# Second attention: where the selection's mask joins each head's bias, a matmul into the logits or an accumulating transfer into the bias

## The chip, the cores and the metric

The kernel runs on one core of one Trainium2 chip. The metric is the device time of one execution, in microseconds; three runs of the kernel before gave 1299.54 to 1299.88 us, median 1299.84.

## The reference, cut to what matters

The model is two layers of a decoder trunk over 512 positions and 1024 features. Layer 0 mixes with a stick-breaking attention, layer 1 with a sparse attention (the "second attention" here), and a gated MLP with a short convolution follows each. In the second attention an indexer scores every key for every query, the 128 best keys are selected, and 16 heads attend to these alone, all with the same keys, with a relative bias of their own and the same selection:

```python
_, sel = lax.top_k(isc, topk)
valid = sel <= t[None, :, None]
...
logits = jnp.einsum('bqhd,bqkd->bqhk', qb, kg) * scale
bias = rel_bias[t5_bucket(t[None, :, None] - sel)]
logits = logits + jnp.swapaxes(bias, -1, -2).astype(jnp.float32)
logits = jnp.where(valid[:, :, None, :], logits, NEG)
p = jax.nn.softmax(logits, axis=-1)
return jnp.einsum('bqhk,bqkd->bqhd', p, vg)
```

The kernel gathers nothing: it computes the logits against all keys up to the query's block, adds the bias, and adds -1e30 where a key is not selected, so the softmax gives those keys 0.

## The kernel before, in words

**Tiles.** Queries lie in four blocks of 128 (index j, 0 to 3); block j sees the first (j + 1) * 128 keys, so a head's logits are four tiles of 128, 256, 384 and 512 columns, kept side by side in one tile `L` of 1280 columns (`LOFF` gives the offsets 0, 128, 384, 768). Most matmuls are done three times, with weights and activations each split into a high and a low part (`hi`, `lo`), which ScalarE (ACT) makes by a copy and VectorE (DVE) by a subtraction.

**The mask.** While the queries of the first 12 heads are projected, DVE takes the top 128 keys by repeated max and match-replace (`topk_steps`), and at the end (L1205) writes `maskb`: bf16, 0 or -1e30, the same for all heads.

**The bias.** The relative bias of a head depends only on the distance between query and key, so a row of 640 numbers per head lies in DRAM (`rb`), and `load_bias` (L1325) reads it with overlapping rows, one DMA on the queue of SyncE (SP) of 128 x 512 floats, into a tile `th`. `th` holds the bias in reversed order of keys, and is read backwards. There are two `th` buffers in a pool that opens with the attention part.

**One head.** `logits(h, j)` (L1336) makes tile `z`: three matmuls of queries and keys and, as the fourth (L1346), the identity `ident_b` times `maskb`, which adds the mask in PSUM. `softmax(h, j)` (L1348) has DVE compute `L = z * rq + bias` (L1354) and the negated row maximum `nm` (L1356). `expo(h, j)` has ACT take the exponential, with the row's sum. `transposed(h, .)` turns `L` on TensorE (PE) in three pieces (tile `tr`), copied out to `pT` by ACT or DVE. `weighted(h)` multiplies two heads' weights with the values (`av`), once for every pair of heads; `pair_sums`, `pair_scale`, `pair_hi`, `pair_lo` scale that pair's result and split it. There are two PSUM banks for `z`, two for `tr`, one for the small products (`x`), three for projections.

**The order.** The program's order is written by hand, and every engine runs its own instructions in it. The loop over heads h does the logits and the softmax of head h + 1 between the transposes of head h: first `logits(h+1, 0)` and `(h+1, 1)`, then (even h above 0) `weighted(h-2)`, the first transposes of head h, some steps of other work (`fill`: projections of the last four heads' queries, then half of the output projection, with their splits as `events`), `logits(h+1, 2)`, more transposes, `logits(h+1, 3)`, the last transposes, and at the end of the head the load of the bias of head h + 2. In the text, tile (n, j) means block j of head n.

**The weights.** All weights come through a ring of six buffers of 128 x 1024 floats, pool `raws`. `fetch` (through `chunk_raw`, L178) issues their loads on SP's queue, one chunk ahead of the split. SP's queue is in order: a transfer that waits for its buffer holds up all that stand behind it.

**GpSimd (POOL)** does, before the attention part, the low halves of 12 splits (`wlo`), and nothing in it.

Of the kernel before, what the change touches and what calls it, by code (L numbers as in the profile page):

```python
# [9 lines left out]
F32 = mybir.dt.float32  # L10
F32R = mybir.dt.float32r
BF = mybir.dt.bfloat16
AF = mybir.ActivationFunctionType
OP = mybir.AluOpType
# [4 lines left out]
D = 1024  # L19
S = 512  # L20
P = 128
KT = D // P
QT = S // P
# [4 lines left out]
HEADS = 16  # L28
# [10 lines left out]
LATE_STEPS = [2, 3, 2, 3, 3, 3, 3, 3, 3, 3, 5, 5, 5, 5, 5, 8]  # L39
AHEAD = 2  # L40
FETCH = 1
IDXFILL = [1, 1, 1, 0, 1, 1, 1, 1]

TRP = [[(0, 0)], [(1, 0), (3, 384)], [(2, 0)]]
TRW = [512, 512, 256]
LOFF = [0, 128, 384, 768]
LW = 1280
# [71 lines left out]
def kernel_body(ctx, tc, xT, wst, cst, smalls, crow, ccol, relb, onehot, outT):  # L119
    nc = tc.nc  # L120
    act, dve, pe, pool = nc.scalar, nc.vector, nc.tensor, nc.gpsimd
# [927 lines left out]
    def dsa_layer(l, first, man):  # L1049
        with ExitStack() as st:  # L1050
# [233 lines left out]
            with ExitStack() as sa:  # L1284
# [34 lines left out]
                def fill(n):  # L1319
                    for _ in range(n):  # L1320
                        next(filler, None)
                        if events:
                            events.pop(0)()

                def load_bias(h):  # L1325
                    th = ths[h] = ap.tile([P, S], F32, name="th", bufs=2)
                    ov = rb[h:h + 1, 0:1]
                    nc.sync.dma_start(th, bass.AP(tensor=ov.tensor, offset=ov.offset, ap=[[1, P], [1, S]]))

                def begin(h):  # L1330
                    L = ap.tile([P, LW], F32, name="L")
# [5 lines left out]
                def logits(h, j):  # L1337
                    qh, ql = Q[h]
                    ns = (j + 1) * P
                    qs = slice(j * P, ns)  # L1340
                    ls = slice(LOFF[j], LOFF[j] + ns)
                    z = heads[h][4][j] = ptile([P, S], "z", "z")
                    pe.matmul(z[:, :ns], lhsT=qh[:, qs], rhs=kph[:, :ns], start=True, stop=False)
                    pe.matmul(z[:, :ns], lhsT=ql[:, qs], rhs=kph[:, :ns], start=False, stop=False)
                    pe.matmul(z[:, :ns], lhsT=qh[:, qs], rhs=kpl[:, :ns], start=False, stop=False)
                    pe.matmul(z[:, :ns], lhsT=ident_b, rhs=maskb[:, ls], start=False, stop=True)  # L1346

                def softmax(h, j):  # L1348
                    L, nm, sum_, rv, z = heads[h]
                    z = z.pop(j)  # L1350
                    ns = (j + 1) * P
                    ls = slice(LOFF[j], LOFF[j] + ns)
                    c = h * QT + j
                    dve.scalar_tensor_tensor(L[:, ls], z[:, :ns], rq[:, c:c + 1], ths[h][:, :ns][:, ::-1],  # L1354
                                             op0=OP.mult, op1=OP.add)
                    dve.tensor_reduce(nm[:, j:j + 1], L[:, ls], axis=AX.X, op=OP.max, negate=True)  # L1356

                def expo(h, j):
                    L, nm, sum_ = heads[h][:3]
                    ls = slice(LOFF[j], LOFF[j] + (j + 1) * P)  # L1360
                    act.activation(L[:, ls], L[:, ls], AF.Exp, bias=nm[:, j:j + 1], accum_out=sum_[:, j:j + 1])
# [74 lines left out]
                for j in range(QT):  # L1436
                    logits(0, j)
                    fill(1)
                    softmax(0, j)
                    expo(0, j)  # L1440
                rvb = None

                def sums(h):
# [4 lines left out]
                for h in range(HEADS):  # L1448
                    n = h + 1
                    more = n < HEADS  # L1450
                    values = h % 2 == 0 and h > 0
                    if more:
                        begin(n)
                        for j in range(2):
                            logits(n, j)
                        softmax(n, 0)
                        expo(n, 0)
# [25 lines left out]
                    if more:  # L1483
                        softmax(n, 3)
                        expo(n, 3)
                        if n + 1 < HEADS:
                            load_bias(n + 1)
                    else:
                        pair_scale(rvb)
                    fill(LATE_STEPS[h] - LATE_STEPS[h] // 2)  # L1490
# [124 lines left out]
```

## Time and profile before

| | us |
|---|---|
| median of three runs | 1299.84 |
| span of the profiled execution (first to last instruction) | 1297.7 |
| the second attention's loop over heads, about | 771 to 903 of the span |
| PE busy over the span | 1280.5 |
| DVE busy over the span | 930.7 |
| ACT busy over the span | 591.4 |
| POOL busy over the span | 35.8 |

The profile is of one execution. The page's own times are in us from the start of its span; the runs' times are 2.1 us longer than that span. A row of the timeline gives the start, the duration, the engine, the line of the kernel, the operation, "out<-in", the shapes and, in brackets, how long the engine had stood idle before it and what released it. PEld is PE's loading of weights, which overlaps PE's matmuls. Matmuls are pipelined: what one costs is read from the start of the next, not from its own duration. In the chain of waits each row is a start, a length and the instruction that the end of the program waited for at that time.

### The profile page before, as it was taken

Reading aid. Unit: us, or ns where it says so; the run is one execution under the profiler, and the core shown is the slowest. Engines: PE = TensorE matmul, PEld = TensorE weight load, DVE = VectorE, ACT = ScalarE, POOL = GpSimd, SP = SyncE. Lnnn points to the kernel's source line nnn. Section 1 sums busy time; section 2 is a strip of 40 time slices with the busy share of each in tenths; the row PEclk is TensorE's granted clock in tenths of the full one; section 3 lists DMA queues with packets and bytes.
Section 4 is the critical chain, followed back from the end, with each engine's and each line's share of the span. In section 5 each row is a group of like instructions: output and inputs, shape, how many; then the busy total and the mean of one; then the engine's idle time right before and its main releaser. Section 6 shows DMA issues by size and latency. Waiting matters only on the chain.

```text
span 1297.7 us, 18005 instructions
## 1 busy us (share of the span) xinstructions
PE 1280.5 (99%) x6988; PEld 1066.7 (82%) x6988; DVE 930.7 (72%) x1532; ACT 591.4 (46%) x1049; POOL 35.8 (3%) x27
## 2 busy tenths in 40 slices
PE   8999999999999999999999999999999999999998
PEld 5978787898888888888987777777998888888888
DVE  5888988778777877875778877777876456456643
ACT  5476666454323423442555346565554234234430
POOL 0000000000000000000102410000000000000000
PEclk9999999999999999999999999999999999999999
DMA  9644444324575575654213211213222422423221
GB/s 375 207 130 131 144 126 125 126 66 124 199 252 191 175 246 190 192 175 142 80 52 91 88 31 51 65 58 122 82 83 78 129 86 74 129 91 97 73 90 66
DMA packets 50613, 163.23 MB, mean 126 GB/s; under 512 B 5808, under 2 KB 8624, under 8 KB 50528
## 3 DMA queue, kind: packets, MB, share of 16 engines
q1 hardware_dynamic: 50096, 161.30, 38.6%
q8 instruction: 55, 0.90, 0.3%
q10 hardware_dynamic: 432, 0.79, 0.2%
q14 instruction: 30, 0.25, 0.1%
HBM read 159.92 MB, written 2.14 MB: 125 GB/s over the span
## 4 chain that ended last, share of the span: by engine, by line
PE 92%; DVE 3%; ACT 2%; DMA 1%; issue 1%; SPq 0%; DVEq 0%; ACTq 0%
PE pt_u L249 11%; PE pt_u L250 11%; PE pt_u L251 11%; PE pt_d L250 5%; PE pt_d L249 5%; PE pt_d L251 5%; PE pt_first L250 2%; PE pt_l L249 2%; PE pt_first L251 2%; PE pt_first L249 2%; PE pt_l L250 2%; PE pt_l L251 2%; PE pt_q L249 2%; PE pt_q L251 2%; PE pt_q L250 2%; PE pt_qk L249 2%
## 5 line engine op out<-in xcount | busy, mean ns | idle before, releaser
L209 ACT ACTIVATE whi<-raw 128x1024 fp32r<-128x1024 f32 (+1 forms) x206 | 205.2, 1002 | 118.8 <-PE pt_d L251 89.6
L249 PE MATMUL pt_u<-hhi,whi 128*128 128x512 f32 x640 | 249.4, 390 | 0.0
L250 PE MATMUL pt_u<-hhi,wlo 128*128 128x512 f32 x640 | 249.2, 389 | 0.0
L251 PE MATMUL pt_u<-hlo,whi 128*128 128x512 f32 x640 | 249.1, 389 | 0.0
L217 DVE TENSOR_TENSOR wlo<-raw,whi 128x1024 fp32r<-128x1024 f32 (+1 forms) x194 | 223.7, 1154 | 17.7 <-ACT whi L209 16.8
L985 ACT ACTIVATE y<-pt_u,sm 128x512 f32<-128x512 f32 x80 | 62.2, 777 | 188.3 <-PE pt_u L251 188.3
L249 PEld LDWEIGHTS pt_u<-hhi,whi 128*128 128x128 f32 x640 | 120.2, 188 | 26.0 <-issue 1.1
L251 PEld LDWEIGHTS pt_u<-hlo,whi 128*128 128x128 f32 x640 | 120.2, 188 | 24.9
L250 PEld LDWEIGHTS pt_u<-hhi,wlo 128*128 128x128 f32 x640 | 120.2, 188 | 24.7
L986 DVE SCALAR_TENSOR_TENSOR y<-pt_u,sm,y 128x511 f32<-128x511 f32 x80 | 59.9, 749 | 97.0 <-ACT y L985 96.8
L249 PE MATMUL pt_d<-acthi,whi 128*128 128x512 f32 x288 | 112.1, 389 | 0.0
L251 PE MATMUL pt_d<-actlo,whi 128*128 128x512 f32 x288 | 112.1, 389 | 0.0
L250 PE MATMUL pt_d<-acthi,wlo 128*128 128x512 f32 x288 | 112.1, 389 | 0.0
L258 DVE SCALAR_TENSOR_TENSOR raw<-raw,cond 128x1024 f32<-128x1024 f32 x88 | 106.6, 1217 | 3.8 <-DMA raw<-wst 3.8
L360 DVE SCALAR_TENSOR_TENSOR x<-pt_d,mod,x 128x512 f32<-128x512 f32 x48 | 36.0, 750 | 72.8 <-PE pt_d L251 72.8
L233 ACT ACTIVATE acthi<-y 128x512 fp32r<-128x512 f32 x44 | 27.8, 632 | 105.4 <-DVE y L1004 105.4
L249 PE MATMUL pt_first<-hhi,whi 128*128 128x256 f32 (+1 forms) x224 | 68.6, 306 | 0.1
L250 PE MATMUL pt_first<-hhi,wlo 128*128 128x256 f32 (+1 forms) x224 | 67.2, 300 | 0.9 <-DVE wlo L217 0.8
L251 PE MATMUL pt_first<-hlo,whi 128*128 128x256 f32 (+1 forms) x224 | 67.0, 299 | 0.0
L249 PEld LDWEIGHTS pt_d<-acthi,whi 128*128 128x128 f32 x288 | 54.1, 188 | 11.2
L251 PEld LDWEIGHTS pt_d<-actlo,whi 128*128 128x128 f32 x288 | 54.1, 188 | 11.2
L250 PEld LDWEIGHTS pt_d<-acthi,wlo 128*128 128x128 f32 x288 | 54.1, 188 | 11.2
(253 smaller groups left out, 2661.3 us busy)
## 6 DMA issues: line engine op xcount, KB each, us to landing
raw<-wst SPq DMA_DIRECT2D x250, 512.0 KB, 3.7
raw<-wst SPq DMA_DIRECT2D x48, 384.0 KB, 3.0
th<-rb SPq DMA_DIRECT2D x16, 256.0 KB, 3.5
ada<-wst SPq DMA_DIRECT2D x4, 512.0 KB, 6.3
outT<-x SPq DMA_DIRECT2D x16, 128.0 KB, 1.7
x<-xT SPq DMA_DIRECT2D x5, 256.0 KB, 5.0
x<-xT ACTq DMA_DIRECT2D x3, 256.0 KB, 3.9
cond<-crow SPq DMA_DIRECT2D x1, 512.0 KB, 10.5
```

Source lines behind the costliest of these rows:

```text
L209: act.activation(hi[:, :n], raw[:, :n], AF.Copy)
L217: engine.tensor_sub(lo[:, :n], raw[:, :n], hi[:, :n].bitcast(F32))
L233: act.activation(hi, src, AF.Copy)
L249: pe.matmul(out, lhsT=whi, rhs=ahi, start=start, stop=False)
L250: pe.matmul(out, lhsT=wlo, rhs=ahi, start=False, stop=False)
L251: pe.matmul(out, lhsT=whi, rhs=alo, start=False, stop=stop)
L258: dve.scalar_tensor_tensor(raw, raw, 1.0, cond, op0=OP.mult, op1=OP.mult, accum_out=dst)
L360: dve.scalar_tensor_tensor(x[f][:, c], pt, mod[l][:, g * KT + f:g * KT + f + 1], x[f][:, c], op0=OP.mult, op1=OP.add)
L985: act.activation(y, pt, AF.Identity, scale=cw[2], bias=sm[:, b + S_CB + c:b + S_CB + c + 1])
L986: dve.scalar_tensor_tensor(y[:, 1:], pt[:, :S - 1], cw[1], y[:, 1:], op0=OP.mult, op1=OP.add)
```

## The change

For heads 2 to 15 the mask is no longer added by PE. After head 0's exponentials, `store_mask` has ACT copy the mask, reversed and as floats, into two tiles, and stores them in DRAM (`maskd`). The bias of such a head is loaded in four pieces, one for each block j, into two tiles of the ring `raws` (blocks 0 to 2 in one of 768 columns, block 3 in one of 512), so that it lies as the mask lies; then two DMAs on POOL's queue add `maskd` onto the two tiles as they transfer. Heads 0 and 1 keep the matmul, and their bias, 128 x 512, comes into the ring as well. The pool of two `th` buffers is gone. The load for head h + 2 stands at the beginning of head h, not at its end.

```diff
+PEMASK = 2
...
+                maskd = dp.tile([P, LW], F32, name="maskd")
+
+                def halves_of():
+                    return [raws.tile([P, D], F32, name="th", tag="raw")[:, :w] for w in (LOFF[3], S)]
+
+                def store_mask():
+                    for t, c0 in zip(halves_of(), (0, LOFF[3])):
+                        for j in (0, 1, 2) if c0 == 0 else (3,):
+                            ns = (j + 1) * P
+                            act.activation(t[:, LOFF[j] - c0:LOFF[j] - c0 + ns], maskb[:, LOFF[j]:LOFF[j] + ns][:, ::-1], AF.Copy)
+                        nc.sync.dma_start(maskd[:, c0:c0 + t.shape[1]], t)
+
                 def load_bias(h):
-                    th = ths[h] = ap.tile([P, S], F32, name="th", bufs=2)
+                    th = ths[h] = halves_of() if h >= PEMASK else halves_of()[1:]
                     ov = rb[h:h + 1, 0:1]
-                    nc.sync.dma_start(th, bass.AP(tensor=ov.tensor, offset=ov.offset, ap=[[1, P], [1, S]]))
+                    for j in range(QT) if h >= PEMASK else (3,):
+                        ns = (j + 1) * P
+                        t = th[-1] if j == 3 else th[0][:, LOFF[j]:LOFF[j] + ns]
+                        nc.sync.dma_start(t, bass.AP(tensor=ov.tensor, offset=ov.offset, ap=[[1, P], [1, ns]]))
+                    if h >= PEMASK:
+                        pool.dma_start(th[0], maskd[:, :LOFF[3]], accum_op=OP.add)
+                        pool.dma_start(th[1], maskd[:, LOFF[3]:], accum_op=OP.add)
...
-                    pe.matmul(z[:, :ns], lhsT=qh[:, qs], rhs=kpl[:, :ns], start=False, stop=False)
-                    pe.matmul(z[:, :ns], lhsT=ident_b, rhs=maskb[:, ls], start=False, stop=True)
+                    pe.matmul(z[:, :ns], lhsT=qh[:, qs], rhs=kpl[:, :ns], start=False, stop=h >= PEMASK)
+                    if h < PEMASK:
+                        pe.matmul(z[:, :ns], lhsT=ident_b, rhs=maskb[:, ls], start=False, stop=True)
...
-                    dve.scalar_tensor_tensor(L[:, ls], z[:, :ns], rq[:, c:c + 1], ths[h][:, :ns][:, ::-1],
+                    dve.scalar_tensor_tensor(L[:, ls], z[:, :ns], rq[:, c:c + 1], bias_of(h, j),
...
+                store_mask()
                 rvb = None
...
                     values = h % 2 == 0 and h > 0
+                    if n + 1 < HEADS:
+                        load_bias(n + 1)
                     if more:
                         begin(n)
...
                         expo(n, 3)
-                        if n + 1 < HEADS:
-                            load_bias(n + 1)
```

**PE, in the loop of head 6**, from the small product `ssq` to the logits of tile (7, 2). First before, then now:

```order
L1091 MATMUL ssq<-ecols,q_7760 128x1 x4
L1343 MATMUL z<-kph,qh 128x128
L1344 MATMUL z<-kph,ql 128x128
L1345 MATMUL z<-kpl,qh 128x128
L1346 LDWEIGHTS ident_b
L1346 MATMUL z<-maskb,ident_b 128x128
L1343 MATMUL z<-kph,qh 128x256
L1344 MATMUL z<-kph,ql 128x256
L1345 MATMUL z<-kpl,qh 128x256
L1346 LDWEIGHTS ident_b
L1346 MATMUL z<-maskb,ident_b 128x256
L1372 MATMUL tr<-cons,L 128x128 x4
```

The same stretch of PE after the change, where the lines of the code have moved on by some 26:

```order
L1092 MATMUL ssq<-ecols,q_7793 128x1 x4
L1369 MATMUL z<-kph,qh 128x128
L1370 MATMUL z<-kph,ql 128x128
L1371 MATMUL z<-kpl,qh 128x128
L1369 MATMUL z<-kph,qh 128x256
L1370 MATMUL z<-kph,ql 128x256
L1371 MATMUL z<-kpl,qh 128x256
L1399 MATMUL tr<-cons,L 128x128 x4
```

Of PE nothing moved but the mask's weight loads and matmuls, 56 of each, which are gone.

**SP, at the start of the attention part**, from the first bias on (`th` with a number is one tile; heads 0, 1, 2, 3 in this order; in brackets the engines and DMA semaphores that the transfer waits for). First before, then now:

```order
L1328 DMA th_7175<-rb_102 128x512 [waits DVE_49,DMAHW1_49,PE_49,Activation_49]
L1328 DMA th_7177<-rb_102 128x512 [waits DMAHW2_49]
L1328 DMA th_7289<-rb_102 128x512 [waits DMAHW3_49,DMAHW1_49,DVE_49]
L1328 DMA th_7373<-rb_102 128x512 [waits DMAHW4_49,DMAHW2_49,DVE_49]
L1328 DMA th_7453<-rb_102 128x512 [waits DMAHW5_49,DMAHW3_49,DVE_49]
```

The same place of SP after the change:

```order
L1345 DMA th_7177<-rb_102 128x512 [waits DMAHW1_49,Pool_49]
L1345 DMA th_7180<-rb_102 128x512 [waits DMAHW2_49,Pool_49]
L1337 DMA maskd_7175<-th_7230 128x768 [waits DMAHW3_49,Activation_49]
L1337 DMA maskd_7175<-th_7231 128x512 [waits DMAHW4_49,Activation_49]
L1345 DMA th_7238<-rb_102 128x128 [waits DMAHW5_49,DMAHW1_49,DVE_49]
L1345 DMA th_7238<-rb_102 128x256 [waits DMAHW6_49]
L1345 DMA th_7238<-rb_102 128x384 [waits DMAHW7_49]
L1345 DMA th_7239<-rb_102 128x512 [waits DMAHW3_49,DMAHW0_49,Pool_49]
```

The first two loads no longer wait for DVE, PE and ACT but for POOL, and between them and the loads for head 2 stand now the two stores of the mask, which wait for ACT.

More of the change, by code (lines that the diff above doesn't have):

```diff
@@ L1323, in fill, with bias_of @@
                             events.pop(0)()
+                maskd = dp.tile([P, LW], F32, name="maskd")
[7 more added lines that the diff above has]
+                        nc.sync.dma_start(maskd[:, c0:c0 + t.shape[1]], t)
                 def load_bias(h):
-                    th = ths[h] = ap.tile([P, S], F32, name="th", bufs=2)
+                    th = ths[h] = halves_of() if h >= PEMASK else halves_of()[1:]
                     ov = rb[h:h + 1, 0:1]
-                    nc.sync.dma_start(th, bass.AP(tensor=ov.tensor, offset=ov.offset, ap=[[1, P], [1, S]]))
+                    for j in range(QT) if h >= PEMASK else (3,):
[5 more added lines that the diff above has]
+                        pool.dma_start(th[1], maskd[:, LOFF[3]:], accum_op=OP.add)
+                def bias_of(h, j):
+                    ns = (j + 1) * P
+                    if j == 3 or h < PEMASK:
+                        return ths[h][-1][:, :ns][:, ::-1]
+                    return ths[h][0][:, LOFF[j]:LOFF[j] + ns][:, ::-1]
                 def begin(h):
```

## The prediction

> **What bounds the kernel now.** I read the page first, then the busy times by stretches of the attention loop, then PE's timeline there.
>
> ```profile
> span 1297.7 us, 18005 instructions
> ...
> 800.00:816.00 16.00, 16.00 (x107) 12.61 (x107) 12.58 (x25) 10.22 (x29) 0.00 (x0) 1.00 0.11 32
> 816.00:834.00 18.00, 17.04 (x113) 13.09 (x113) 13.08 (x28) 10.37 (x29) 0.00 (x0) 1.00 0.21 61
> ```
>
> The columns of the stretches are length, then PE, PEld, DVE, ACT, POOL busy, granted clock, DMA share, GB/s. PE is full in two heads (16.00 of 16.00 us) and loses one microsecond in the next two; DVE follows with 13 of 16 to 18, POOL is empty. So PE bounds the stage, with a chain through DVE and ACT close behind. What a mask matmul costs is the distance to the next start:
>
> ```profile
> 809.17 0.23 PE L1346 MATMUL z<-maskb,ident_b 128*128 128x128 bf16 x1
> 809.21 0.36 PE L1343 MATMUL z<-kph,qh 128*128 128x256 f32 x1
> ...
> 809.65 0.28 PE L1346 MATMUL z<-maskb,ident_b 128*128 128x256 bf16 x1
> 809.77 0.60 PE L1372 MATMUL tr<-cons,L 128*128 128x128 f32 x4
> ...
> 811.44 0.34 PE L1346 MATMUL z<-maskb,ident_b 128*128 128x384 bf16 x1
> 811.62 0.60 PE L1372 MATMUL tr<-cons,L 128*128 128x128 f32 x4
> ...
> 812.75 0.39 PE L1346 MATMUL z<-maskb,ident_b 128*128 128x512 bf16 x1
> 812.98 1.05 PE L1387 MATMUL pv<-uvc,latf 128*128 128x128 f32 x8
> ```
>
> That is 0.04, 0.12, 0.18 and 0.23 us for blocks 0 to 3, 0.57 us a head, 8.0 us for 14 heads. This is the most that the removal can give.
>
> **What of the 8.0 us reaches the end.** The loop repeats every two heads. After `weighted` PE makes tile (n, 2) and DVE, idle until then, starts; from there DVE runs almost without a gap until `weighted` comes again. Where PE waits for that chain, a mask removed before the wait gives nothing. Waits of PE for it, and near misses, in order of time:
>
> ```profile
> PE z L1343 <- DVE L L1354: 2.8, 3, 1.4
> ...
> 793.97 0.33 PE L1372 MATMUL tr<-cons,L 128*128 128x128 f32 x1 [0.29 <-ACT L L1361]
> ...
> 820.87 0.62 DVE L1354 SCALAR_TENSOR_TENSOR L<-z,cols,th 128x384 f32<-128x384 f32 x1 [3.31 <-PE z L1346]
> ...
> 828.11 0.44 PE L1343 MATMUL z<-kph,qh 128*128 128x384 f32 x1 [0.96 <-DVE L L1354]
> ...
> 832.00 0.74 DVE L1354 SCALAR_TENSOR_TENSOR L<-z,cols,th 128x512 f32<-128x512 f32 x1
> ...
> 833.11 0.36 PE L1343 MATMUL z<-kph,qh 128*128 128x256 f32 x1
> ...
> 846.96 0.55 ACT vals L1391 x2
> 847.56 1.05 PE ssq L1091 x8
> ...
> 866.53 0.74 DVE L1354 SCALAR_TENSOR_TENSOR L<-z,cols,th 128x512 f32<-128x512 f32 x1
> ...
> 867.48 0.36 PE L1343 MATMUL z<-kph,qh 128*128 128x256 f32 x1
> ```
>
> The first row is from the list of waits (total, times, longest); 846.96 and 847.56 are from the chain of waits, which there runs on DVE and ACT from the start of the pair. A pair, from one DVE start after `weighted` to the next, holds the masks of blocks 3; 0, 1, 2, 3; 0, 1, 2 (0.23 + 0.57 + 0.34 = 1.14 us). There are six pairs:
> - 789.8 to 805.7: PE already waits 0.29 us at 793.97 for the last exponential, so blocks 3, 0, 1 before it (0.39) are lost: 0.74.
> - 805.7 to 820.9: PE is full (the first stretch above): 1.1.
> - 820.9 to 838.2: PE waits 0.96 us at 828.11, so the same 0.39 is lost. After that the end of DVE's (n, 3) at 832.74 leaves 0.37 us to PE's start at 833.11, just what blocks 2, 3 and 0 save there (0.45): about 0.7.
> - 838.2 to 855.3: the chain reaches 847.56, behind all but the last three masks: 0.04 + 0.12 + 0.18 = 0.35.
> - 855.3 to 873.2: 867.48 - 867.27 = 0.21 us of room, a little more as DVE's small gaps close; then 0.12 + 0.18: 0.6.
> - 873.2 to 891.9: the third of the three waits (2.8 less 1.4 and 0.96) is here, at the same place as in the third pair: 0.7.
>
> With block 2 of head 3 (0.18) and block 3 of head 15 (0.23) that is 4.6 us. What lies before, head 2 and the rest of head 3, is swallowed by the next part.
>
> **The start: a wait that goes.** Before, the first bias waited for the attention part's pool.
>
> ```profile
> L1289 SPq DMA_DIRECT2D uvc<-wst x4: 376/424/430, 735.2 to 736.6; - x4
> ...
> L217 POOL TENSOR_TENSOR wlo<-raw,whi x1: 2412/2412/2412, 755.8 to 755.8; 128x1024 fp32r<-128x1024 f32 x1
> ...
> 763.56 0.80 SPq L1328 DMA_DIRECT2D th<-rb  x2
> 764.84 0.19 DVE L1126 TENSOR_SCALAR cols<-cols 128x48 f32<-128x48 f32 x1
> 766.75 0.35 DVE L1354 SCALAR_TENSOR_TENSOR L<-z,cols,th 128x128 f32<-128x128 f32 x1 [1.72 <-DMA th<-rb]
> 767.15 0.44 PE L1343 MATMUL z<-kph,qh 128*128 128x384 f32 x1 [1.37 <-DVE L L1354]
> ```
>
> It left at 763.56, and DVE stood 1.72 us. In the ring it waits only for POOL's splits, the last over at 758.2, and SP has nothing left ahead of it since 737. So it lands in time and DVE starts 1.7 us earlier, PE's wait of 1.37 us at 767.15 with it. I take 1.7.
>
> **The start: a wait that comes.** Head 2 needs the mask in DRAM first. ACT's copies stand between its exponentials:
>
> ```profile
> 772.01 0.39 ACT L1361 ACTIVATE L<-L,nm 128x128 f32<-128x128 f32 x1
> ...
> 775.17 0.62 ACT L1361 ACTIVATE L<-L,nm 128x384 f32<-128x384 f32 x1 [0.59 <-DVE nm L1356]
> ...
> 777.21 0.72 ACT L1361 ACTIVATE L<-L,nm 128x512 f32<-128x512 f32 x1 [1.07 <-DVE nm L1356]
> ...
> L1377 ACT ACTIVATE pT<-tr 128x512 f32<-128x512 f32 x16 | 9.4, 589 | 10.0 <-PE tr L1372 10.0
> ...
> th<-rb SPq DMA_DIRECT2D x16, 256.0 KB, 3.5
> ...
> raw<-wst SPq DMA_DIRECT2D x48, 384.0 KB, 3.0
> ```
>
> The four copies have 1280 columns; by a copy of 512 in 0.59 us, 1.4 us. ACT's idle times of 0.59 and 1.07 us just behind hide them (without that cover: 1.4 us). On a clock already 1.7 us early: free at 772.0 - 1.7 = 770.3, copies done 771.7, the stores and then three loads for head 2 leave at 0.4 us each (0.80 for two, above), the last at 772.8; it lands 3.0 to 3.5 us later, at 776.1. The larger store, 384 KB, takes about 3.0 us like a load of that size and is down by then. Then POOL's transfer starts; call its time A. No row shows one. It brings 384 KB and must also read what it adds to: not less than a plain transfer (3.0), not more than two in a row (6.0), if nothing else slows it. I take the middle, A = 4.5, as both readings share one latency. So DVE gets the bias of head 2 at T = 776.1 + 4.5 = 780.6.
>
> By the Trainium skill, "DMA: Bandwidth & Descriptors", section "Anatomy of one DMA — SWDGE (gpsimd) path", a transfer from GpSimd takes 2.0 us + bytes/436e3, and by its "Collectives: The Full Stack", section "The bandwidth ceiling: the fold count and why AG ≠ RS ≠ AR", an adding transfer reads two sources at half the rate; together an estimate of 2.0 + 2 x 0.9 = 3.8 us, and a sum 0.7 us lower. The row of 3.0 us agrees with the first for a plain transfer; the second no run here shows.
>
> ```profile
> 777.69 0.34 DVE L1354 SCALAR_TENSOR_TENSOR L<-z,cols,th 128x128 f32<-128x128 f32 x1
> ...
> 780.74 0.62 DVE L1354 SCALAR_TENSOR_TENSOR L<-z,cols,th 128x384 f32<-128x384 f32 x1 [0.41 <-PE z L1346]
> ...
> 783.00 0.75 DVE L1354 SCALAR_TENSOR_TENSOR L<-z,cols,th 128x512 f32<-128x512 f32 x1
> ...
> 784.74 0.36 PE L1343 MATMUL z<-kph,qh 128*128 128x256 f32 x1
> ...
> 785.39 2.37 PE L1404 MATMUL av<-pT,vals 128*64 128x512 f32 x16
> ```
>
> On the early clock DVE would want it at 777.69 - 1.7 = 776.0. It waits, PE's next `z` wait behind it, and DVE runs from T without a gap: (2, 0) to (2, 3) took 783.00 - 777.69 = 5.31 us, 0.41 of it a wait that goes, so 4.9, plus 0.75 for (2, 3); then PE's tile (3, 1), 785.39 - 784.74 less its mask, 0.53. `weighted(0)` starts at T + 6.2 = 786.8, against 785.39: 1.4 us late, the 1.7 us included.
>
> **In the loop.** The four loads and two transfers of a head must be over when DVE wants them; block 2 of head h frees the buffer of head h + 2 at the earliest (heads 6, 9, 12, 15), otherwise it is free sooner. The tightest of these in an odd pass:
>
> ```profile
> 795.74 0.62 DVE L1354 SCALAR_TENSOR_TENSOR L<-z,cols,th 128x384 f32<-128x384 f32 x1
> ...
> 809.47 0.34 DVE L1354 SCALAR_TENSOR_TENSOR L<-z,cols,th 128x128 f32<-128x128 f32 x1
> ```
>
> Head 6: free at 796.4, wanted at 809.47, 13.1 us; three issues (1.1), landing (3.5) and A take 4.6 + A = 9.1. Four microseconds cover it. In SP's queue the weights' loads now stand behind these; they are one chunk ahead of their split, by one head or more, so I cost that at nothing; without that cover it is one landing, some 3.5 us, once a pair.
>
> **Sum.** +1.4 - 4.6 = -3.2 us on the span: 1294.5; with the 2.1 us between span and median, 1296.6 us. In general A - 7.7.
>
> **Rivals.**
> - *PE is the bound everywhere and the transfer is as fast as a plain one.* For it: PE full in 800 to 816. Against it: the waits at 793.97 and 828.11. A = 3.0 puts `weighted(0)` at -0.1, and 7.3 us of masks follow: -7.4, 1292.4 us.
> - *The chain through DVE and ACT binds in every pair*, as at 847.56. For it: DVE's long runs without a gap. Against it: the full stretch. Six times 0.35 and 0.41 make 2.5; +1.4 - 2.5 = -1.1, 1298.7 us.
> - *POOL's transfers start late because of DVE.* Two of DVE's instructions of about 0.7 us ahead of each make A = 5.9: -1.8, 1298.0 us. For it: DVE is busy 13 of 16 us; against it: it stands idle, waiting, when the first one starts. The Trainium skill's "SBUF — State Buffer", section "SBUF: two separate sides", speaks so against this change: descriptors written by GpSimd wait while VectorE holds the shared port in a two-port copy, 620 ns growing to 3100 ns; no run here shows it.
> - *The adding transfer is slow, A about 10 us, and the kernel gets slower.* Place: the wait of DVE for head 2, then head 6. 10 - 7.7 = +2.3, and head 6 waits 4.6 + 10 - 13.1 = 1.5: +3.8, 1303.6 us. For it: no row bounds such a transfer from above but my 6.0. Against it: all other transfers of this size land in 3 to 4 us. It decides slower from A = 9.4.
>
> **How the numbers follow.** About 0.2%, 2.6 us, is what a measurement of this kernel can tell from no change. Forecast 0.48, of which 0.08 lies within 2.6 us, since A above 5.1 does that; first rival 0.12, second 0.15, third 0.08, fourth 0.17. Faster 0.40 + 0.12 = 0.52; same 0.08 + 0.15 + 0.08 = 0.31; slower 0.17. The range goes from the first rival's 1292.4 to 1301.5, which is A of about 9; beyond lies most of the fourth rival and little of the first.
>
> **What would show it.** L1346 eight times instead of 64; DVE's first `L` near 765.0; a wait of DVE for the DMA of `th` of some 4 us before tile (2, 0), and PE behind it; no such wait in heads 3 to 15; `weighted(0)` near 786.8 and the loop's end some 3 us earlier than 903. The forecast is wrong if waits for `th` come in the loop, if PE's waits for DVE and ACT don't grow, or if the first 1.7 us don't come.

## The result, and the profile after

| | us |
|---|---|
| before, median of four runs | 1299.69 |
| after, median of four runs (1309.27 to 1313.4) | 1310.64 |
| ratio after to before, with its 95% interval | 1.0087 [1.0072, 1.0101] |
| span of the profiled execution, after | 1307.5 |

The changed kernel is slower by 11 us; 1296.6 was forecast, and the range ended at 1301.5. The profiled run, 1309.27 us, is the fastest of its four. One of the eleven executions of kernel 3 below took 2578.14 us, against 1297.4 to 1298.45 for the others; its cause is not known, and the ratio leaves it out. I begin with the same stretches of the loop, and one more where the loop starts (columns as above: length, PE, PEld, DVE, ACT, POOL busy, granted clock, DMA share, GB/s).

```profile
773.00:785.00 12.00, 3.94 (x26) 3.21 (x24) 2.46 (x5) 3.21 (x8) 1.98 (x3) 0.81 0.87 135
...
800.00:816.00 16.00, 15.38 (x101) 12.52 (x100) 13.45 (x28) 10.95 (x32) 3.46 (x4) 1.00 0.91 190
816.00:834.00 18.00, 15.57 (x98) 11.89 (x96) 11.47 (x25) 9.18 (x27) 3.49 (x4) 1.00 0.94 196
```

The first of these stretches before:

```profile
773.00:785.00 12.00, 11.50 (x75) 9.46 (x74) 9.93 (x20) 7.87 (x23) 0.00 (x0) 1.00 0.09 29
```

Two things are new. From 773 to 785 us PE works 4 us of 12, where it worked 11.5: one large hole. And the DMA engines, 0.11 and 0.21 busy before in the last two stretches, are now 0.91 and 0.94 busy, at under 200 GB/s. The hole is at head 2, in the rows of SP, POOL, DVE and PE:

```profile
764.46 0.35 DVE L1381 SCALAR_TENSOR_TENSOR L<-z,cols,th 128x128 f32<-128x128 f32 x1
768.89 0.34 DVE L1381 SCALAR_TENSOR_TENSOR L<-z,cols,th 128x128 f32<-128x128 f32 x1
...
770.77 0.84 SPq L1337 DMA_DIRECT2D maskd<-th  x2
771.71 2.51 SPq L1345 DMA_DIRECT2D th<-rb  x5
...
780.09 1.01 POOL L1347 DMA_DIRECT2D th<-maskd  x1 [22.53 <-DMA th<-rb]
...
786.97 0.35 DVE L1381 SCALAR_TENSOR_TENSOR L<-z,cols,th 128x128 f32<-128x128 f32 x1 [11.47 <-DMA th<-maskd]
...
787.37 0.69 PE L1369 MATMUL z<-kph,qh 128*128 128x384 f32 x1 [9.76 <-DVE L L1381]
...
793.95 0.65 PE L1431 MATMUL av<-pT,vals 128*64 128x512 f32 x2
```

DVE's first step comes early, at 764.46, so the start gain is there. Then the mask's stores leave at 770.77, head 2's loads behind them from 771.71, the first adding transfer at 780.09, and DVE has its bias at 786.97, after 11.47 us of standing; PE stands 9.76 us behind it. `weighted(0)` starts at 793.95, against 785.39 before. Later in the loop DVE waits for a bias again, above all before tiles (7, 0) and (9, 0); the last row is its step (15, 3):

```profile
829.07 0.35 DVE L1381 SCALAR_TENSOR_TENSOR L<-z,cols,th 128x128 f32<-128x128 f32 x1 [5.41 <-DMA raw<-wst]
...
846.86 0.35 DVE L1381 SCALAR_TENSOR_TENSOR L<-z,cols,th 128x128 f32<-128x128 f32 x1 [3.73 <-DMA th<-maskd]
...
903.38 0.72 DVE L1381 SCALAR_TENSOR_TENSOR L<-z,cols,th 128x512 f32<-128x512 f32 x1
```

(The profile names a weights' load for the first, which landed last; head 7's adding transfer, issued at 821.14, landed 7.8 us later, at the same time. A third wait, 1.18 us before (12, 0) at 870.73, it puts down to PE; but head 12's adding transfer, issued at 864.96, landed 5.7 us later, just then.) The DMA issues of the page, with KB each and the median time from issue to landing, show how long every link takes:

```profile
th<-maskd POOLq DMA_DIRECT2D x14, 384.0 KB, 6.1
th<-rb SPq DMA_DIRECT2D x16, 256.0 KB, 6.7
th<-maskd POOLq DMA_DIRECT2D x14, 256.0 KB, 7.2
th<-rb SPq DMA_DIRECT2D x14, 192.0 KB, 6.4
```

The same 256 KB of bias took 3.5 us before. In the traces below I use two differences, since the stage as a whole begins up to two microseconds earlier or later from one profile to the next: from DVE's tile (1, 0) to (2, 0), which holds the wait at head 2, and from (2, 0) to (15, 3), which holds the loop. Before they are 777.69 - 771.17 = 6.5 and 893.72 - 777.69 = 116.0 us; after, 786.97 - 768.89 = 18.1 and 903.38 - 786.97 = 116.4 us. The two rows of before for this, (1, 0) and (15, 3):

```profile
771.17 0.34 DVE L1354 SCALAR_TENSOR_TENSOR L<-z,cols,th 128x128 f32<-128x128 f32 x1
```

```profile
893.72 0.74 DVE L1354 SCALAR_TENSOR_TENSOR L<-z,cols,th 128x512 f32<-128x512 f32 x1
```

### The profile page after: what moved, and what is told of

It reads as the page before. It is cut to its first block, busy times and chain, and to the rows that moved or that the text cites. A ratio compares the mean times of both kernels' runs of the same rounds, so it can differ in the third digit from the quotient of the medians.

```text
span 1307.5 us, 18086 instructions
## 1 busy us (share of the span) xinstructions
PE 1275.8 (98%) x6931; PEld 1065.2 (81%) x6932; DVE 930.5 (71%) x1532; ACT 592.7 (45%) x1053; POOL 60.4 (5%) x55
## 4 chain that ended last, share of the span: by engine, by line
PE 89%; DMA 4%; DVE 4%; ACT 2%; issue 1%; SPq 0%; another core or an unknown queue 0%; DVEq 0%; ACTq 0%
PE pt_u L250 11%; PE pt_u L252 11%; PE pt_u L251 11%; PE pt_d L250 5%; PE pt_d L252 5%; PE pt_d L251 5%; PE pt_first L251 2%; PE pt_first L250 2%; PE pt_first L252 2%; PE pt_l L250 2%; PE pt_l L251 2%; PE pt_l L252 2%; PE pt_q L250 2%; PE pt_q L252 2%; PE pt_q L251 2%; DMA th<-maskd 2%
```

## The experiments

Four theories. **Theory 1:** the adding transfers fill the DMA engines, by their bytes (1a) or because adding reads the destination as well (1b). **Theory 2:** most of the loss occurs once, at head 2, where nothing hides the chain from the mask to its first use. **Theory 3:** the ring's buffers come free late, so the bias loads start late. **Theory 4**, formed from kernels 9 and 10: head 2's loads stand behind the mask's store on SP's queue. All results in one table; times are medians, ratios are to the kernel before on the same chip, and the last two columns are the differences above, from each profiled run.

| kernel | us | ratio [95%] | (1,0) to (2,0) | (2,0) to (15,3) |
|---|---|---|---|---|
| before | 1299.69 | | 6.5 | 116.0 |
| after | 1310.64 | 1.0087 [1.0072, 1.0101] | 18.1 | 116.4 |
| 1 no adding transfers | 1294.34 | 0.9956 [0.9944, 0.9969] | 7.3 | 111.1 |
| 2 one load, no mask | 1294.24 | 0.9951 [0.9937, 0.9964] | 6.5 | 111.1 |
| 3 one load, mask on PE | 1298.29 | 0.9985 [0.9976, 0.9994] | 6.5 | 116.0 |
| 4 copies in place of adds | 1308.36 | 1.0066 [1.0053, 1.0078] | 16.6 | 115.7 |
| 5 adds from head 4 on | 1303.41 | 1.0027 [1.0016, 1.0038] | 6.9 | 123.4 |
| 6 block 3 alone added | 1306.61 | 1.0053 [1.0041, 1.0065] | 7.2 | 124.9 |
| 7 own tiles for block 3 | 1311.66 | 1.0087 [1.0074, 1.0100] | 20.1 | 113.7 |
| 8 adds by GpSimd itself | 1294.00 | 0.9956 [0.9943, 0.9969] | 6.5 | 111.6 |
| 9 mask read from SBUF | 1295.46 | 0.9963 [0.9949, 0.9976] | 6.6 | 113.7 |
| 10 adds in head 2 alone | 1308.18 | 1.0067 [1.0054, 1.0080] | 16.2 | 116.2 |
| 11 long rows | 1300.44 | 1.0001 [0.9992, 1.0011] | 12.6 | 112.4 |
| 12 block 3 from head 4 on | 1295.99 | 0.9972 [0.9961, 0.9983] | 7.0 | 114.0 |
| 13 head 2's loads first | 1306.27 | 1.0045 [1.0031, 1.0059] | 10.9 | 123.5 |
| 14 both 10 and 13 | 1303.24 | 1.0026 [1.0016, 1.0036] | 12.0 | 116.8 |

**1. Without the adding transfers.**

```diff
-                    if h >= PEMASK:
-                        pool.dma_start(th[0], maskd[:, :LOFF[3]], accum_op=OP.add)
-                        pool.dma_start(th[1], maskd[:, LOFF[3]:], accum_op=OP.add)
```

> The after kernel without its 28 adding transfers: heads 2 to 15 get no mask at all (the mask is still stored to DRAM, the bias still comes in four pieces into the ring, early). Theory 1 (the adding transfers fill the DMA engines, and that is what made the kernel slower): with them gone the loads land in 3 to 4 us, DVE's first steps of the heads wait for no transfer, and the kernel keeps the start gain of 1.7 us and the 4.6 us of the mask matmuls: 1299.7 - 1.7 - 4.6 = 1293.4 us. Rival (the bias tiles in the ring and the four-piece loads are what comes late, not the adds): no faster than before, 1300 us or more. Rival on the size (the mask matmuls are worth all of their 8.0 us): 1290.0 us.

1294.34 us, within a microsecond of theory 1's number, and the rival (ring and four-piece loads alone make the kernel slow) falls. With the adds 16.3 us come: by the traces 18.1 - 7.3 = 10.7 us once at head 2, 116.4 - 111.1 = 5.3 us in the loop. But theory 1 is too simple in one part: the loads in four pieces take most of the DMA engines' time before any add does. The engines were 0.11 busy in this stretch before, 0.91 in the after kernel, and here, without adds, 0.69:

```profile
800.00:816.00 16.00, 15.98 (x107) 12.92 (x104) 13.25 (x29) 9.03 (x29) 0.00 (x0) 1.00 0.69 130
```

**2 and 3. One load per bias, without and with the mask's matmul.**

```diff
-                    for j in range(QT) if h >= PEMASK else (3,):
+                    for j in (3,):
...
-                store_mask()
```

Both also lose the adds and the tile of blocks 0 to 2; the second has `PEMASK = 16` besides.

> No mask for heads 2 to 15, no store, no adding transfers, and each bias again as one load of 128x512, in the ring and at the early place. This is the gain without any of its price: the mask matmuls gone (56 of them) and the start earlier by 1.7 us. If the mask matmuls are worth the 4.6 us that the prediction took: 1293.4 us. If all of their 8.0 us reach the end: 1290.0 us. If the chain DVE-ACT sets every pair: 1297.5 us or more. Beside the kernel without the adds it prices the four-piece loads: equal within 0.5 us if those are hidden.

> The before kernel with the bias tiles in the ring and each load issued at the head's start; the mask is still added by the matmul in every head, so nothing is left out. If the 1.7 us that DVE's first step of head 0 gains go through to the end: 1298.0 us. If the gained time is lost to the next wait in the stage: 1299.7 us, no change.

The kernel with the matmuls kept and only the loads early takes 1298.29 us: of the start gain 1299.75 - 1298.29 = 1.46 us come through. Without the matmuls it is 1294.24: these were worth 4.05 us (by the traces 116.0 - 111.1 = 4.9 us), close to the 4.6 of the prediction, not all 8.0. Kernels 1 and 2 are equal within 0.1 us, so four-piece loads cost no time where no add stands behind them.

**4. Copies in place of adds.**

```diff
-                        pool.dma_start(th[0], maskd[:, :LOFF[3]], accum_op=OP.add)
+                        pool.dma_start(th[0], maskd[:, :LOFF[3]])
```

(and so for the second).

> The after kernel with its 28 adding transfers made plain copies of the same tiles on the same queue (the bias of heads 2 to 15 is overwritten by the mask). Theory 1a (it is the bytes and the extra traffic, whatever the transfer does): the landings stay at 6 to 8 us and the time near the after kernel's, 1307 to 1311 us. Theory 1b (it is the adding, which has to read its destination and so moves at half the rate): the copies take about 2 us of the 16 engines a head in place of 3.8, land in about 4 us, and the time falls to about 1298 us (only a wait at head 2 left).

The DMA queues over the loop (queue, packets, MB, share of 16 engines), of the after kernel from 768 to 903 us:

```profile
q1 hardware_dynamic: 9504, 14.03, 46.6%
q0 software_dynamic: 4032, 9.18, 39.7%
```

and of this kernel in the same window, with a row of its page on the landings and one of its timeline at tile (7, 0):

```profile
q0 software_dynamic: 2240, 9.18, 20.9%
```

```profile
th<-maskd POOLq DMA_DIRECT2D x14, 384.0 KB, 4.4
```

```profile
828.72 0.35 DVE L1381 SCALAR_TENSOR_TENSOR L<-z,cols,th 128x128 f32<-128x128 f32 x1 [5.73 <-DMA th<-maskd]
```

The same bytes need half of the engines' time as copies: 0.397 x 135 us / 14 = 3.8 us of all 16 engines a head as adds, 2.0 as copies. Yet the kernel wins only 2.3 us, and the waits stay: the step at head 2 still takes 16.6 us, and there is one again at tile (7, 0). So 1b is true of the transfer and explains little of the time.

**5. Adds from head 4 on.** `PEMASK = 4`.

> The after kernel with the mask by the matmul in heads 0 to 3 and by adding transfers from head 4 on (nothing is left out). By the traces, DVE's first step of head 2 came 18.1 us after that of head 1 in the after kernel and 7.3 us after it where the adds were left out: 10.7 us once; from there to the last head's step it took 116.4 us against 111.1: 5.3 us spread over the loop. Theory 2 (two thirds of the loss is a wait that occurs once, for the first chain of store, load and add, with no head's work to hide it): with two heads ahead of the first add the 10.7 us go, some of the 5.3 stay, and 2 of 14 heads' mask matmuls (0.6 us) come back: 1310.6 - 10.7 + 0.6 = 1300.5 us, less if the loop's waits go too (1295.5 at best). Theory 1 (the DMA engines can't carry 1.25 MB a head in the heads' time, so the wait only moves to head 4): 1308 us or more.

1303.41 us, between the two (its runs spread from 1299.69 to 1309.14). The wait at head 2 is gone, but one of the same kind has moved to head 7, with smaller ones before (9, 0) and (15, 0), 2.47 and 3.13 us:

```profile
822.23 0.35 DVE L1381 SCALAR_TENSOR_TENSOR L<-z,cols,th 128x128 f32<-128x128 f32 x1 [9.40 <-DMA th<-maskd]
```

Around it the loads issued from 802.9 to 810 us land after 5 to 10 us, a weight's load of 512 KB after 9.3, and head 7's first add after 9.7: three heads' transfers lie in the queues at once. Theory 2 is right for head 2 and not the whole story. In the loop the wait does move, as theory 1 had it, though to head 7 and not to 4, and short of its 1308 us.

**6. Only block 3 by an adding transfer.**

```diff
-                        pool.dma_start(th[0], maskd[:, :LOFF[3]], accum_op=OP.add)
...
-                    if h < PEMASK:
+                    if h < PEMASK or j < 3:
```

> The after kernel with the mask added by a transfer in block 3 alone (256 KB a head); blocks 0 to 2 get it by the matmul again (nothing is left out). Of the 4.05 us that the mask matmuls were worth, block 3 has 0.23 of 0.57, 1.6 us. Block 3 is wanted some 5 us after the head's first block. If the wait is one of the chain load, then add: the start wait falls from 10.7 to about 5 us and the loop's waits mostly go: 1298.3 - 1.6 + 5 = 1301.7 us. If the DMA engines' load in the loop is what costs: it falls from 1.25 to 0.9 MB a head, and the time to half way, about 1303 us.

1306.61 us, above both numbers that were expected: two fifths of the adds' bytes (256 of 640 KB) keep three fifths of the loss (1306.61 against 1296.7 without waits, where the after kernel has 1310.64 against 1294.34). Most of it is at tile (2, 3):

```profile
790.61 0.75 DVE L1380 SCALAR_TENSOR_TENSOR L<-z,cols,th 128x512 f32<-128x512 f32 x1 [7.64 <-DMA th<-maskd]
```

That one add left at 781.64, 0.6 us later than the same add in the after kernel, and landed after 8.9 us. Two waits for head 2's loads, 0.61 and 1.19 us, stand before it, and PE, after standing 7.97 us behind it, ran at a granted clock of 0.50 until 797.4. No wait for a transfer over 0.3 us follows in the loop. This speaks for theory 2.

**7. Tiles of its own for block 3.**

```diff
-                    return [raws.tile([P, D], F32, name="th", tag="raw")[:, :w] for w in (LOFF[3], S)]
+                    return [raws.tile([P, D], F32, name="th", tag="raw")[:, :LOFF[3]], ap.tile([P, S], F32, name="th3", bufs=2)]
```

> The after kernel with the bias tiles of block 3 in two buffers of their own; only the tile of blocks 0 to 2 and the weights still share the ring of six (nothing is left out). Theory 3 (loads start late since the ring's buffers come free late, and that makes the waits at heads 7 and 9): the loop's 5.3 us go for the most part: 1306 us. Theory 1 (the engines are full): no change, 1310 us. The wait at head 2 stays in both.

No gain. The loop does lose half of its waits (113.7 against 116.4, and no wait at head 7), so theory 3 has a share there; but the first bias waits for the pool again (1.93 us before tile (0, 0)), and the wait at head 2 grows by 2.0 us.

**8. The mask added by GpSimd itself.**

```diff
-                        pool.dma_start(th[0], maskd[:, :LOFF[3]], accum_op=OP.add)
-                        pool.dma_start(th[1], maskd[:, LOFF[3]:], accum_op=OP.add)
+                        for j in range(QT):
+                            ns = (j + 1) * P
+                            t = th[-1] if j == 3 else th[0][:, LOFF[j]:LOFF[j] + ns]
+                            pool.tensor_tensor(t, t, maskb[:, LOFF[j]:LOFF[j] + ns][:, ::-1], op=OP.add)
...
-                store_mask()
```

> The after kernel with the mask added to the bias tiles by four instructions a head on GpSimd, reading the mask on chip, in place of the two adding transfers; no store of the mask, no DRAM copy (nothing is left out). Estimate from the 128x1024 pass of 2.4 us on GpSimd in the trace of before: 1280 columns a head, 3 us. If only the transfers were the trouble: the first head's add takes about 1 us past its load, and the rest is hidden: 1294.3 + 1 = 1295.3 us. If GpSimd's passes slow DVE beside them, or take over 8 us a head: 1300 us or more.

POOL's group in the loop, and DVE's first step of head 2:

```profile
L1350 POOL TENSOR_TENSOR th<-th,maskb 128x512 f32<-128x512 f32 (+3 forms) x53 | 46.1, 877 | 68.6 <-DMA th<-rb 66.5 <-DVE bs L1453 1.8 <-DVE nm L1385 0.2
```

```profile
776.21 0.34 DVE L1383 SCALAR_TENSOR_TENSOR L<-z,cols,th 128x128 f32<-128x128 f32 x1
```

1294.00 us: faster than both kernels, and equal to the kernel that adds no mask at all. Four instructions of 877 ns on average, 3.5 us a head, lie on an engine that had nothing to do, and DVE waits for no transfer. The removal of the matmul was worth its 4 us all along; only the way in which the mask reached the bias was dear.

**9. The mask tile kept in SBUF, as bf16.**

```diff
-                maskd = dp.tile([P, LW], F32, name="maskd")
+                maskd = ap.tile([P, LW], BF, name="maskd", bufs=1)
...
-                            act.activation(t[:, LOFF[j] - c0:LOFF[j] - c0 + ns], maskb[:, LOFF[j]:LOFF[j] + ns][:, ::-1], AF.Copy)
-                        nc.sync.dma_start(maskd[:, c0:c0 + t.shape[1]], t)
+                            act.activation(maskd[:, LOFF[j]:LOFF[j] + ns], maskb[:, LOFF[j]:LOFF[j] + ns][:, ::-1], AF.Copy)
```

> The after kernel with the mask kept on chip: the four copies on ScalarE write a reversed bf16 mask tile of 128x1280 in SBUF, there is no store to DRAM, and the 28 adding transfers read that tile (half the bytes of the source, none of them from DRAM) and add it to the fp32 bias tiles (nothing is left out). If the adding transfer's price lies in what it reads: it lands in 4 us or less in place of 6 to 7, the share of the DMA engines falls, and the time to 1304 us or so. If its price lies in the adding itself or in the pieces that it is cut into: no faster than the after kernel, 1309 us or more. The store is no link of the chain (it was through 6 us before the first add), so its loss alone should give nothing.

1295.46 us, far below what either side expected, though all 28 adding transfers are there. From the timeline of SP, POOL and DVE, and the queue's row from 771 to 900 us:

```profile
743.42 14.87 SPq L1344 DMA_DIRECT2D th<-rb  x6
```

```profile
771.71 1.01 POOL L1346 DMA_DIRECT2D th<-maskd  x1 [13.77 <-ACT maskd L1336]
```

```profile
775.91 0.35 DVE L1380 SCALAR_TENSOR_TENSOR L<-z,cols,th 128x128 f32<-128x128 f32 x1
```

```profile
q0 software_dynamic: 4032, 9.18, 30.5%
```

The six loads from 743 to 758 us are those of heads 0 and 1 and the four of head 2. With no store on SP's queue the last of them leaves 13 us before the first would have left behind it, the first add goes out as soon as ACT's copies are done, at 771.71, and DVE's step at 775.91 waits for nothing. My sentence in the expectation, that the store is no link of the chain, was wrong: it was no link by its duration, but by its place in the queue. This kernel changes more than that, though: the source is on chip and half as long, and the mask takes no buffer of the ring; kernels 13 and 14 change the order. In the loop, half of the waits are gone too (113.7): the engines' share of the adds fell from 39.7 to 30.5%.

**10. Adding transfers for head 2 alone** (`h == PEMASK` in place of `h >= PEMASK`; the others load 128x512 once and have the matmul).

> Adding transfers and four-piece loads for head 2 alone; heads 3 to 15 have the mask by the matmul and one load of 128x512 as before (nothing is left out). This prices the first chain of store, load and add with quiet DMA engines. With the prediction's terms (load 3.0 to 3.5 us, add 4.5 us) DVE's first step of head 2 comes 1.4 to 2 us late: 1298.3 - 0.3 + 1.7 = 1299.7 us. With the landings of the after kernel (7 and 7 us), if those don't come from the traffic of the other heads: 10 us late, 1308 us. In between, about 1303 us, if head 3's loads were half of the cause.

```profile
780.73 1.00 POOL L1347 DMA_DIRECT2D th<-maskd  x1 [22.69 <-DMA th<-rb]
```

```profile
785.58 0.35 DVE L1381 SCALAR_TENSOR_TENSOR L<-z,cols,th 128x128 f32<-128x128 f32 x1 [9.60 <-DMA th<-maskd]
```

1308.18 us: one head's chain costs 10 us (1298.0 without it, by the expectation's terms), as much as head 2's wait does in the after kernel. With few other transfers under way the add itself took 4.8 us, close to the prediction's A = 4.5; but it left at 780.73, as late as in the after kernel. What is late is what stands ahead of the add.

**11. Long rows.** The bias tiles get their bytes in rows of 3072 and 2048 bytes:

```diff
-                    for j in range(QT) if h >= PEMASK else (3,):
-                        ns = (j + 1) * P
-                        t = th[-1] if j == 3 else th[0][:, LOFF[j]:LOFF[j] + ns]
-                        nc.sync.dma_start(t, bass.AP(tensor=ov.tensor, offset=ov.offset, ap=[[1, P], [1, ns]]))
+                    for t in th:
+                        nc.sync.dma_start(t, wst[CH["uv",], :, :t.shape[1]])
```

> The after kernel with each bias tile loaded in one transfer of the same bytes, 128 rows of 3072 and of 2048 bytes from a weight (the bias of all heads is replaced by these numbers), in place of four transfers with overlapping rows of 512 to 2048 bytes; the adding transfers are as they were. If the small rows make the loads slow (67 GB/s at 774 to 777 us in the after kernel's neighbour without adds): the loads land in 3 to 4 us, the start wait falls by 3 to 4 us, and with the loop's waits gone it takes about 1302 us. If only the bytes count: 1309 us or more.

Packets and rate in the microsecond from 774 to 775, first of the after kernel, where only four-piece loads run (head 2's and the first of head 3's), then of this one:

```profile
DMA packets 86, 0.06 MB, mean 55 GB/s; under 512 B 6, under 2 KB 86, under 8 KB 86
```

```profile
DMA packets 115, 0.32 MB, mean 322 GB/s; under 512 B 10, under 2 KB 10, under 8 KB 115
```

About as many packets pass in a microsecond, with a sixth of the bytes. The first add leaves at 776.51 in place of 780.09, and the loop is down to 112.4 us, 1.3 above the kernel without adds. 1300.44 us, somewhat below the first forecast: the short rows cost 10 us here, by the traces 5.5 at head 2 and 4.0 in the loop, though without adds behind them they cost nothing. The edit also makes two transfers out of four and ends the overlap of the rows; which of the three counts was not separated.

**12. Block 3 alone, from head 4 on** (kernels 5 and 6 together).

> The mask of block 3 by an adding transfer from head 4 on, everything else by the matmul (nothing is left out; half the adds' bytes, and two heads of time ahead of the first). Theory 2 (the loss of the kernel with block 3 alone from head 2 on was the one wait at its first add): no wait is left, and 12 of the 16 block-3 mask matmuls are saved, 1.4 us: 1298.3 - 1.4 = 1296.9 us. Theory 1 (the four-piece loads and the weights bunch up whatever the adds do, and the wait moves to head 7 as in the kernel with all adds from head 4): 1301 us or more.

1295.99 us, theory 2's number; no wait for a transfer over 0.5 us is left. Against kernel 6 two more heads of time ahead of the first add are worth 10.6 us.

**13 and 14. Head 2's loads ahead of the store**, in the after kernel and in kernel 10; `add_mask` holds the two adding transfers.

```diff
+                load_bias(PEMASK)
                 store_mask()
...
-                        load_bias(n + 1)
+                        if n + 1 != PEMASK:
+                            load_bias(n + 1)
+                        add_mask(n + 1)
```

> The after kernel with head 2's four loads issued ahead of the mask's store instead of behind it; its adding transfers stay where they were (nothing is left out). Theory 4 (head 2's loads stood behind the store on SP's queue until 770.8 us, so a chain of three transfers lay between the mask and DVE's step): they leave before 760 us, the first add follows the store (773.3 us) and lands 4.8 us later, 778.1 us, 1.4 to 2 us late in place of 10.7: 1310.6 - 9 = 1301.6 us, the loop's 5.3 us staying. Rival (the adding transfers themselves are slow there): the add lands 7 us or more after it leaves, 781 us, and the time is 1304 us. Rival (the place of the loads doesn't matter): 1309 us or more.

> The kernel with adding transfers in head 2 alone, with head 2's four loads issued ahead of the mask's store (nothing is left out). Theory 4: DVE's first step of head 2 comes 1.4 to 2 us late instead of 9; 1298.3 - 0.3 + 1.7 = 1299.7 us, and the sum that the prediction made for the start holds once the loads are out of the way. Rival (the place of the loads doesn't matter): 1308 us.

Kernel 13, POOL's and DVE's rows, then DVE's of kernel 14:

```profile
775.44 1.01 POOL L1349 DMA_DIRECT2D th<-maskd  x1 [16.10 <-DMA maskd<-th]
```

```profile
781.59 0.35 DVE L1383 SCALAR_TENSOR_TENSOR L<-z,cols,th 128x128 f32<-128x128 f32 x1 [2.97 <-DMA th<-maskd]
```

```profile
782.39 0.35 DVE L1383 SCALAR_TENSOR_TENSOR L<-z,cols,th 128x128 f32<-128x128 f32 x1 [4.02 <-DMA th<-maskd]
```

The first add now follows the store, not the loads, and the step from (1, 0) to (2, 0) falls from 18.1 to 10.9 us and from 16.2 to 12.0: theory 4 accounts for 7 of the 10.7 us in the after kernel and 4 of 9 in the quiet one. Against kernel 1's 7.3 us, 3.6 and 4.7 stay. The add itself, with 6.1 and 7.1 us in place of 4.8, makes 1.3 and 2.3 of them; it now runs beside the second store and the next head's loads. The rest, 2.2 and 2.3, is the chain of store and add at the price of 4.8. The new order also has a price that the expectation didn't see, here in kernel 13: ACT's last copy of the mask, apparently for want of a free buffer in the ring, waits for the first store, all of ACT's work stands behind it, and the second store leaves 3.0 us after the first in place of 0.5:

```profile
774.93 0.63 ACT L1336 ACTIVATE th<-maskb 128x512 f32<-128x512 bf16 x1 [2.40 <-DMA maskd<-th]
```

In time the order is worth 1310.64 - 1306.27 = 4.4 and 1308.18 - 1303.24 = 4.9 us. Both kernels stay above what theory 4 forecast, by 4.7 and 3.5 us; the add's length explains 1.3 and 2.3 of that, and the rest is open. (Both profiled runs, 1310.96 and 1305.23 us, are the slowest of their kernels; their columns are higher than the medians would have.)

## Why the prediction was wrong, step by step

- *What the mask matmuls are worth, 4.6 us:* right, and not by luck. Kernels 3 and 2 give 4.05, the traces 4.9, and pair by pair, from one DVE step (n, 2) to the next, the traces give 0.81, 1.00, 0.62, 0.41, 0.67 and 0.65 us where 0.74, 1.1, 0.7, 0.35, 0.6 and 0.7 were forecast. The first two rivals, with 7.3 and 2.5 us for the masks, fall by this.
- *The start gain of 1.7 us:* right. Kernel 3 gives 1.46.
- *The loads of head 2, "it lands 3.0 to 3.5 us later, at 776.1":* **the first step that failed.** The loads left when forecast, the third at 772.8, but the add that waits for them left at 780.09, 4.0 us later. The 3.5 us was the row of one load of 2048-byte rows on idle engines; here came three of 512 to 1536 bytes, behind 640 KB of stores. The third piece took 6.7 us, and 6.7 and 6.8 in kernels 1 and 10, where no add is under way; in kernel 13 the same piece, long ahead of the stores, took 4.8. Its rows from kernels 10 and 13:

```profile
th<-rb SPq DMA_DIRECT2D x1, 192.0 KB, 6.8
```

```profile
th<-rb SPq DMA_DIRECT2D x1, 192.0 KB, 4.8
```

  So of the 3.2 us above the forecast price the short pieces make 1.3, and what moves just ahead of them and beside them (the stores, head 2's fourth piece, head 3's first) 1.9. Long rows bring the add to 776.51, as forecast. And the order that the prediction saw itself (the stores, "and then three loads for head 2") was priced at three issues of 0.4 us; kernels 9 and 13, where the loads leave before 760, show that it held them back so long that all of their time came after the mask's.
- *A = 4.5 us:* right for quiet engines (4.8, kernel 10), wrong here: 786.97 - 780.09 = 6.9. So T is 787.0 in place of 780.6, and `weighted(0)`, 7.0 us behind it, is at 793.95 in place of 786.8: 7.1 us. That it follows by 7.0 and not 6.2 is PE's doing, which has no gap from 787.37 to 793.95 and ran the first half of that at half the clock (last section).
- *In the loop, "four microseconds cover it":* **the second step that failed.** Both durations in it were too short: 3.5 for the landing was the price of a whole load on engines that were 0.1 to 0.2 busy, and 4.5 for A that of an undisturbed transfer. With the change the engines are 0.9 busy, the medians are 6.4 to 6.7 and 6.1 to 7.2 us, and of the 13.1 us nothing is left. For the loads the form counts more than the adds: their medians are already 5.3 to 5.9 us in kernel 1, without adds, and 3.6 to 3.8 in kernel 11, in long rows beside the adds, which take 5.8 there. The waits at heads 7, 9 and 12 follow, which the prediction had named as a sign that it is wrong. They cost 5.3 us net, and the loop's forecast gain of 4.6 is gone: the last `weighted` is 9.6 us late, 1.1 us more than the first. Its rows before and after:

```profile
900.41 2.37 PE L1404 MATMUL av<-pT,vals 128*64 128x512 f32 x16
```

```profile
910.04 2.37 PE L1431 MATMUL av<-pT,vals 128*64 128x512 f32 x16
```

- *The sum:* 1296.6 + 7.1 at head 2 + 5.7 in the loop = 1309.4; the profiled run took 1309.27.
- *The rivals:* the fourth, the slow add, had the sign and the place (head 2, then a later head) and 0.17 of the chance. Its mechanism was only in part what happened: A was 6.9 us and not 10, and it had everything ahead of the add at the old price, so its 1303.6 was too low. That loads in short pieces are slow by themselves, and that loads and adds slow each other, was in no rival, though the bytes could be counted: per head 640 KB of loads and 640 KB of adds where 256 KB were before. The third rival has no part at head 2, where the load's landing released the add and DVE stood idle; in the loop no run separates it.

What stays open is the split of the loop's 5.3 us. Long rows take 4.0 of it away, the mask in SBUF 2.7, tiles of its own 2.7, copies 0.7; these overlap, and no run separates them.

## What to carry to other kernels

A transfer that takes over an engine's work is priced in the form and with the engines' load that it will have after the change, not with the landing times of before: add up the bytes, the rows' length and what an add reads twice, per pass of the loop. Of a step that appears in a queue, look at what stands behind it: here a store that waited for its data held back loads that could have left 13 us earlier or more. And ask whether an idle engine can do the work in place: GpSimd's 3.5 us a head gave the whole gain that the transfers lost.

## What the runs showed of the hardware that was not expected

- An adding transfer from DRAM takes 1.9 times the DMA engines' time of a copy of the same bytes (39.7 and 20.9% of the loop, rows above). The Trainium skill, "Collectives: The Full Stack", section "The bandwidth ceiling: the fold count and why AG ≠ RS ≠ AR", says of the adding step of a ring collective that it needs two source reads and so runs at half the copy's rate; these rows, of a transfer within one core, agree.
- Loads with overlapping rows of 512 to 1536 bytes passed, in the microsecond shown, at about 90 packets and 55 GB/s, against 115 packets and 322 GB/s in long rows.
- A hole in PE's work slows what comes after it. Stretches of 2 us of the after kernel, the granted clock third from the end:

```profile
778.00:780.00 2.00, 0.00 (x0) 0.00 (x0) 0.00 (x0) 0.00 (x0) 0.00 (x0) 1.00 0.97 195
780.00:782.00 2.00, 0.00 (x0) 0.00 (x0) 0.00 (x0) 0.00 (x0) 1.91 (x2) 0.62 1.00 189
...
788.00:790.00 2.00, 2.00 (x9) 1.81 (x8) 1.97 (x4) 1.26 (x6) 0.00 (x0) 0.50 1.07 197
790.00:792.00 2.00, 2.00 (x13) 1.78 (x13) 1.93 (x6) 0.95 (x3) 0.00 (x0) 0.82 0.66 93
```

PE stopped at 777.6; the clock was at 0.50 from 780.5 and back at 790.7, 3.3 us after PE resumed at 787.4, so PE lost up to 1.7 us more. The kernels with shorter or no holes (before, 1, 2, 3, 8, 9 and 12) kept 1.00 through the whole loop; in the loops of the others the low stretches last 3.4, 6.8, 10.2 or 13.7 us, and in kernel 6 the clock came back only 6 us after PE did. The Trainium skill, "TensorE: Matmul & The Clock Gate", section "Part 1: The HAM clock gate (the "warmup" mystery)", has half the clock after an idle window of about 3.4 us, and full again after a busy one as long. The lengths here are multiples of that window, though the clock fell 2.9 us after PE's last matmul.
